# Feed-forwards of a decoder trunk: seven rounds for eight, the order of the block products, and where the second matrix's weights are loaded

## The chip, the core and the metric

One NeuronCore of a Trainium2 chip runs the whole kernel in one launch. The time is the device time of one execution in microseconds (us), and smaller is better. The engines are named as in the profile: PE multiplies matrices, PEld loads its weights, DVE, ACT and POOL work on vectors, SP issues most of the transfers.

## The reference, cut to what matters

The program is one step of a two-layer decoder trunk for 512 prompt tokens and 32 sample tokens. Each layer holds two feed-forwards around a mixer, so there are four in all; the mixers, the shared keys and values and the conditioning are not touched by the change.

```python
def swiglu(u, w_up, w_down):
    a, b = jnp.split(u @ w_up, 2, axis=-1)
    return (jax.nn.silu(a) * b) @ w_down
...
u = modulate(h, P['g_norm'][layer, 0], mod[:, 0, 0], mod[:, 0, 1])
h = h + 0.5 * mod[:, 0, 2][:, None, :] * swiglu(u, P['w_ffn_up'][layer, 0], P['w_ffn_down'][layer, 0])
```

The model width is 1024, the width between the two matrices is 2816, that is 22 columns of 128; all data are float32.

## The kernel before, in words

**Layout.** Activations lie transposed, features on the partitions, in eight blocks of 128 features by 544 tokens. The tokens are taken in two halves of 272. Every operand of a matmul is split into a high part (an ACT cast) and a low part (a DVE subtraction), and each product is three matmuls: high by high, high by low, low by high. The helpers `halves` (line 157 and 158) and `acc3` (lines 176 to 178) do this, so nearly all of these instructions carry those lines; the tiles tell them apart: `p` is a bank of a block product, `pd` a bank of the second matrix, `pa` and `pb` banks of the plain way.

**One feed-forward.** `ffn_seven` is called four times ("00", "02", "10", "12" in time order). A "pair" q is the 128 columns of a and the 128 columns of b that belong together. The first three pairs (0 to 2) are computed plainly. From pair 3 on, `seven` computes a 2 by 2 block product (feature half by token half) with seven products of 12 matmuls each instead of eight, from sums of weights (S1 to S4) and sums of activations (T1 to T4). The sums of activations are made by DVE and ACT while PE works on the plain pairs (`inputs`, `last_input`); T2 and T4 are the tiles `th`, `tl`, and T3 is written over a quarter of `uh`, `ul`.

**Weights of the first matrix.** `load(q)` issues two transfers of 512 KB into the four `raw` buffers (`rua`, `rub`). `stage(q, 0..4)` turns them into operands: step 0 is two POOL operations (lines 639 and 640), step 1 splits A11 and A12 and lets POOL make two more sums, steps 2 to 4 split the summed blocks. Split operands lie in six `hi` and six `lo` buffers. During pair q the steps of pair q + 1 are emitted, between the products of pair q, and `load(q + 2)` behind step 3.

**The second matrix.** The finished pairs (`gh`, `gl`, five or six buffers, parameter `slots`; "00" and "02" have five) are collected in rounds. While a round's pairs are computed, the 16 blocks (8 feature blocks by 2 token halves) of the round before it are emitted between the products by `between`, spread over n products, n at most 7 times (slots - 3). A block of a round of three pairs is 9 matmuls, of a round of two 6. `residual` then adds the bank onto `h` (DVE, line 398; for the second token half also lines 401 and 403 on DVE and POOL). `down_weights(r, m2)` loads and splits the weights of two feature blocks of round r (`rd`, `hd`, `ld`); `blocks` calls it one group ahead. `low` makes the low part of a finished pair on POOL, in the last round on DVE (line 677).

**The end.** The last round's 16 blocks run alone, all of the first token half, then all of the second. Behind each half come the squares for the norm (ACT line 351, sums on POOL line 355), `stats` (PE line 364), a reciprocal root on DVE, `spread` (PE line 342, `rb`), and `make_u`, the input of the next stage. In "00" and "02" a piece of conditioning work (`held`) is emitted ahead of `stats`. The last feed-forward ends in `store` instead.

**Order.** The source gives an order and so a priority; a planner puts the instructions of each engine into their final order by its own costs and gives out the buffers, so that a line moved in the source moves in a queue only as far as the planner follows. Each engine then runs its queue strictly in order.

Of the kernel before, what the change touches and what calls it, by code (L numbers as in the profile page):

```python
# [27 lines left out]
NQ = FF // P  # L28
# [58 lines left out]
def cols(t, nk, w):  # L87
    return t[:, 0:nk * w].rearrange("p (k c) -> p k c", k=nk)
# [11 lines left out]
def trunk_kernel(ctx: ExitStack, tc: tile.TileContext, a, out, dbg=None, stop=None):  # L100
# [9 lines left out]
    def mm_bank(name):  # L110
        return pp.tile([P, 512], F32, tag="mm", name=name, bufs=5)
# [8 lines left out]
    def raw_tile(name, dt=F32):  # L120
        return wp.tile([P, 1040], dt, tag="raw", name=name, bufs=4)

    def hi_tile(name, dt=F32R):
        return wp.tile([P, 1040], dt, tag="hi", name=name, bufs=6)

    def lo_tile(name, dt=F32R):
        return wp.tile([P, 1040], dt, tag="lo", name=name, bufs=6)
# [28 lines left out]
    def halves(hi, lo, src):  # L156
        S.copy(hi, src)  # L157
        V.tensor_tensor(out=lo, in0=src, in1=hi.bitcast(F32), op=ALU.subtract)  # L158
# [14 lines left out]
    def acc3(ps, steps, first=True, last=True):  # L173
        n = len(steps)
        for i, (wh, wl, xh, xl) in enumerate(steps):
            PE.matmul(ps, lhsT=wh, rhs=xh, start=first and i == 0, stop=False)  # L176
            PE.matmul(ps, lhsT=wh, rhs=xl, start=False, stop=False)  # L177
            PE.matmul(ps, lhsT=wl, rhs=xh, start=False, stop=last and i == n - 1)  # L178
# [136 lines left out]
    for t in range(5):  # L315
        n = P if t < 4 else NS
# [196 lines left out]
    def ffn_seven(name, l, s, gate, after_half, steps=(), final=False, first=None, held=(), slots=6, late=False):  # L513
# [8 lines left out]
            for _ in range(max(total * ticks[0] // n_ticks, min(total, ticks[0], 4)) - (total - len(steps))):  # L522
                steps.pop(0)()
        rounds, q0 = [], 0
        for n in (3, 3, 3, 3, 3, 3, 2, 2):
            rounds.append(list(range(q0, q0 + n)))
            q0 += n
        assert q0 == NQ
        H2 = NB // 2
        with tc.tile_pool(name="ffn" + name, bufs=1) as fp:  # L530
# [52 lines left out]
            def operand(i, kh=0, half=0):  # L583
                if i in th:
                    return th[i], tl[i]
                return quarter(uh, kh, half), quarter(ul, kh, half)
            B11, B21, B22 = operand(0, 0, 0), operand(0, 1, 0), operand(0, 1, 1)
            T1, T2, T3, T4 = operand(1), operand(2), operand(0, 0, 1), operand(4)
# [30 lines left out]
            def load(q):  # L619
                if q < NQ:  # L620
                    raws[q] = [raw_tile(f"ru{x}{name}_{q}") for x in "ab"]
                    for raw, c0 in zip(raws[q], (q * P, FF + q * P)):
                        SP.dma_start(out=cols(raw, NB, P), in_=wu[:, c0:c0 + P].rearrange("(k p) c -> p k c", p=P))

            def stage(q, step):
                if q >= NQ:
                    return
                ra, rb_ = raws[q]
                a11, a12, a21, a22 = ra[:, 0:W4], ra[:, W4:2 * W4], rb_[:, 0:W4], rb_[:, W4:2 * W4]
                o = ops.setdefault(q, {})  # L630

                def pair():
                    return hi_tile(f"hu{name}_{q}_{step}"), lo_tile(f"lu{name}_{q}_{step}")

                def view(t, i):
                    return tuple(x[:, i * W4:(i + 1) * W4].rearrange("p (k c) -> p k c", k=H2) for x in t)
                if step == 0:
                    o["s3"] = tmp.tile([P, 512], F32, tag="w2", name=f"s3{name}_{q}", bufs=1)
                    G.tensor_tensor(out=o["s3"][:], in0=a11, in1=a21, op=ALU.subtract)  # L639
                    G.tensor_tensor(out=a21, in0=a21, in1=a22, op=ALU.add)  # L640
                elif step == 1:
                    t = pair()
                    halves(t[0][:, 0:2 * W4], t[1][:, 0:2 * W4], ra[:, 0:2 * W4])
                    o["A11"], o["A12"] = view(t, 0), view(t, 1)
                    G.tensor_tensor(out=a11, in0=a21, in1=a11, op=ALU.subtract)  # L645
                    G.tensor_tensor(out=a12, in0=a12, in1=a11, op=ALU.subtract)
                elif step == 2:
                    t = pair()
                    halves(t[0][:, W4:2 * W4], t[1][:, W4:2 * W4], o["s3"][:])
                    halves(t[0][:, 0:W4], t[1][:, 0:W4], a11)  # L650
                    o["S2"], o["S3"] = view(t, 0), view(t, 1)
                elif step == 3:
                    t = pair()
                    halves(t[0][:, 0:2 * W4], t[1][:, 0:2 * W4], rb_[:, 0:2 * W4])
                    o["S1"], o["A22"] = view(t, 0), view(t, 1)
                else:
                    t = pair()
                    halves(t[0][:, 0:W4], t[1][:, 0:W4], a12)
                    o["S4"] = view(t, 0)

            def product(q, n, w, x):
                ps = mm_bank(f"p{n}{name}_{q}")
                acc3(ps[:, 0:HA], [(w[0][:, k], w[1][:, k], x[0][:, k], x[1][:, k]) for k in range(H2)])
                return ps[:, 0:HA]

            def part(q, what):
                return tmp.tile([P, HA], F32, tag={"u": "nv", "c": "sq", "a": "acc"}[what[0]], name=f"{what}{name}_{q}", bufs=2 if what[0] == "a" else 3)

            def plus_ps(q, what, ps, x):
                d = part(q, what)  # L670
                V.tensor_tensor(out=d[:], in0=ps, in1=x[:], op=ALU.add)
                return d
# [6 lines left out]
            def seven(q, between):  # L679
                o = ops[q]  # L680
                g_tiles(q)
                stage(q + 1, 0)
                s1 = part(q, "u1")
                S.copy(s1[:], product(q, 1, o["A11"], B11))
                between()
                u2 = plus_ps(q, "u2", product(q, 6, o["S2"], T2), s1)
                between()
                a0 = plus_ps(q, "a0", product(q, 2, o["A12"], B21), s1)
                S.activation(a0[:], a0[:], AF.Silu)
                stage(q + 1, 1)  # L690
                between()
                u3 = plus_ps(q, "u3", product(q, 7, o["S3"], T3), u2)
                stage(q + 1, 2)
                between()
                p5 = product(q, 5, o["S1"], T1)
                c22 = plus_ps(q, "c22", p5, u3)
                u4 = plus_ps(q, "a4", p5, u2)
                between()
                c21 = plus_ps(q, "c21", product(q, 4, o["A22"], T4), u3)
                V.tensor_tensor(out=c21[:], in0=c21[:], in1=a0[:], op=ALU.mult)  # L700
                (t0, t1), (t2, t3_) = HALF
                low(q, t0, t1, c21)
                stage(q + 1, 3)
                load(q + 2)
                between()
                c12 = plus_ps(q, "c12", product(q, 3, o["S4"], B22), u4)
                S.activation(c12[:], c12[:], AF.Silu)
                V.tensor_tensor(out=c12[:], in0=c12[:], in1=c22[:], op=ALU.mult)
                low(q, t2, t3_, c12)
                stage(q + 1, 4)  # L710
                between()


            def down_weights(r, m2):
                if r >= len(rounds) or (r, m2) in down_w:
                    return
                qs = rounds[r]
                n = len(qs)
                src = wd[qs[0] * P:(qs[-1] + 1) * P, 2 * m2 * P:2 * (m2 + 1) * P].rearrange("(q p) c -> p q c", p=P)
                raw = raw_tile(f"rd{name}_{r}_{m2}")  # L720
                SP.dma_start(out=cols(raw, n, 2 * P), in_=src)
                hi, lo = hi_tile(f"hd{name}_{r}_{m2}"), lo_tile(f"ld{name}_{r}_{m2}")
                halves(hi[:, 0:2 * n * P], lo[:, 0:2 * n * P], raw[:, 0:2 * n * P])
                down_w[r, m2] = (cols(hi, n, 2 * P), cols(lo, n, 2 * P))
# [61 lines left out]
            last_input()  # L786
            stage(plain, 3)
            stage(plain, 4)
            load(plain + 1)
            down_weights(0, 0)  # L790
            for r in range(1, len(rounds)):
                todo = blocks(r - 1)
                n, done, gone = min(7 * len(rounds[r]), 7 * (slots - 3)), [0], [0]

                def between():
                    done[0] += 1
                    while gone[0] < min(2 * NB * done[0] // n, 2 * NB):
                        next(todo)
                        gone[0] += 1
                    tick()  # L800
                for q in rounds[r]:
                    seven(q, between)
                for _ in todo:
                    pass
            r = len(rounds) - 1
# [771 lines left out]
    if stop == "kv":  # L1577
        return

    ffn_seven("10", 1, 0, mod(1, 0, 2), after("11", mod(1, 1, 0), mod(1, 1, 1)))  # L1580
    dump("h3", h[:])

# [314 lines left out]
```

## Time and profile before

| what | value |
|---|---|
| median of 3 runs | 2404.79 us (2399.41 to 2405.72) |
| the profiled execution | 2402.91 us, its span 2401.1 us |
| mean granted TensorE clock | 0.980 of full speed |
| PE busy | 2298.5 us, 96% of the span |
| PEld busy | 2141.6 us, 89% |
| DVE busy | 1828.6 us, 76% |
| ACT busy, POOL busy | 982.0 us and 923.0 us |

The span runs from the first to the last instruction; what lies around it is 1.8 us. The times of the rows below are microseconds from the start of the span.

A row of busy time by stretch holds the stretch, its length, then busy us (and instructions) of PE, PEld, DVE, ACT and POOL, the granted clock as a share of full speed, the DMA share and GB/s. The four insides summed there are 100 to 448, 795 to 1152, 1352 to 1672 and 2060 to 2378 us. A timeline row holds start, us, engine, line, operation, output and inputs, shape, count, and in brackets the idle time before it with what ended it.

### The profile page before, as it was taken

To read this page: it belongs to the slowest core of one execution; us is meant where nothing else is said; L and a number is where in the kernel's file an instruction comes from. 1 tells how busy PE (TensorE), PEld (TensorE's weight loads), DVE (VectorE), ACT (ScalarE), POOL (GpSimd) and SP (SyncE) were. 2 spreads that over 40 slices of the span, in tenths; PEclk is the share of its full clock that TensorE was granted. 3 is DMA by queue.
4 is the path that set the end of the run, shared out by engine and by line. 5 is a ranking of instruction groups with operands and counts; after the bars stand their busy time and mean duration, and the time that the engine had idled before them with its cause. 6 is when DMAs were issued, how large, how long until landed. Compare 5 with 4: busy or idle time off the path is not lost. (4 is left out here: it accounts for less than half of the span.)

```text
span 2401.1 us, 49301 instructions
## 1 busy us (share of the span) xinstructions
PE 2298.5 (96%) x19292; PEld 2141.6 (89%) x19292; DVE 1828.6 (76%) x3881; ACT 982.0 (41%) x1831; POOL 923.0 (38%) x960
## 2 busy tenths in 40 slices
PE   7999999998999999999989999999999799999999
PEld 6899999987979999999769999999796479999999
DVE  6887777749556987777795988888757667888887
ACT  3343333444533443333524444434436544444432
POOL 0355544207102365444241355543324212455452
PEclk8999999999999999999999999999899899999999
DMA  8535555322172445555467233332146751233322
GB/s 306 172 124 193 192 187 178 114 69 62 54 219 64 141 129 181 187 174 174 144 203 246 81 104 94 99 94 88 47 111 185 157 164 52 78 104 89 102 84 78
DMA packets 356894, 319.45 MB, mean 133 GB/s; under 512 B 25247, under 2 KB 317949, under 8 KB 356614
## 3 DMA queue, kind: packets, MB, share of 16 engines
q1 hardware_dynamic: 341734, 300.24, 40.0%
q0 software_dynamic: 14928, 16.06, 3.0%
q8 instruction: 152, 2.49, 0.4%
q14 instruction: 80, 0.66, 0.1%
HBM read 298.17 MB, written 18.38 MB: 132 GB/s over the span
## 5 line engine op out<-in xcount | busy, mean ns | idle before, releaser
L178 PE MATMUL pd<-gh,ld 128*128 128x272 f32 x1408 | 408.6, 290 | 3.3 <-DVE ld L158 3.3
L176 PE MATMUL pd<-gh,hd 128*128 128x272 f32 x1408 | 409.2, 291 | 2.5 <-ACT hd L157 2.5
L177 PE MATMUL pd<-gl,hd 128*128 128x272 f32 x1408 | 409.3, 291 | 2.2 <-POOL gl L677 2.2
L176 PE MATMUL p<-uh,hu 128*128 128x272 f32 x1216 | 351.8, 289 | 0.0
L177 PE MATMUL p<-ul,hu 128*128 128x272 f32 x1216 | 350.9, 289 | 0.0
L178 PE MATMUL p<-uh,lu 128*128 128x272 f32 x1216 | 350.8, 288 | 0.0
L158 DVE TENSOR_TENSOR lu<-rua,hu 128x512 fp32r<-128x512 f32 (+1 forms) x228 | 272.2, 1194 | 45.9 <-ACT hu L157 37.7
L157 ACT CAST hu<-rua 128x512 fp32r<-128x512 f32 (+1 forms) x228 | 174.0, 763 | 290.4 <-PE p L177 131.8
L398 DVE SCALAR_TENSOR_TENSOR h<-pd,mods,h 128x240 f32<-128x240 f32 (+1 forms) x512 | 240.5, 476 | 49.7 <-PE pd L178 48.9
L178 PEld LDWEIGHTS pd<-gh,ld 128*128 128x128 f32 x1408 | 268.3, 191 | 3.9 <-DVE ld L158 3.9
L176 PEld LDWEIGHTS pd<-gh,hd 128*128 128x128 f32 x1408 | 268.4, 191 | 3.5 <-ACT hd L157 2.7
L177 PEld LDWEIGHTS pd<-gl,hd 128*128 128x128 f32 x1408 | 268.5, 191 | 3.0 <-POOL gl L677 3.0
L176 PE MATMUL p<-th,hu 128*128 128x272 f32 x912 | 264.5, 290 | 1.8 <-ACT th L157 1.8
L178 PE MATMUL p<-th,lu 128*128 128x272 f32 x912 | 264.2, 290 | 0.0
L177 PE MATMUL p<-tl,hu 128*128 128x272 f32 x912 | 264.0, 290 | 0.2 <-DVE tl L158 0.2
L403 POOL TENSOR_TENSOR h<-h,gs 128x32 f32<-128x32 f32 x256 | 127.9, 499 | 333.9 <-DVE gs L401 333.6
L176 PEld LDWEIGHTS p<-uh,hu 128*128 128x128 f32 x1216 | 229.3, 189 | 6.2 <-issue 2.1
L177 PEld LDWEIGHTS p<-ul,hu 128*128 128x128 f32 x1216 | 229.4, 189 | 0.0
L178 PEld LDWEIGHTS p<-uh,lu 128*128 128x128 f32 x1216 | 228.9, 188 | 0.0
L639 POOL TENSOR_TENSOR s<-rua,rub 128x512 f32<-128x512 f32 x76 | 115.1, 1514 | 244.6 <-DMA rub<-in_w_ffn_up_dram 131.3
L645 POOL TENSOR_TENSOR rua<-rub,rua 128x512 f32<-128x512 f32 x76 | 101.2, 1332 | 225.0 <-DVE lu L158 130.2
L176 PEld LDWEIGHTS p<-th,hu 128*128 128x128 f32 x912 | 172.4, 189 | 6.1 <-ACT th L157 2.0
(543 smaller groups left out, 6007.4 us busy)
## 6 DMA issues: line engine op xcount, KB each, us to landing
adaw<-in_w_ada_dram SPq DMA_DIRECT2D x128, 512.0 KB, 4.5
rua<-in_w_ffn_up_dram SPq DMA_DIRECT2D x88, 512.0 KB, 3.9
rub<-in_w_ffn_up_dram SPq DMA_DIRECT2D x88, 512.0 KB, 3.8
rd<-in_w_ffn_down_dram SPq DMA_DIRECT2D x96, 384.0 KB, 3.3
adah<-in_w_ada_dram SPq DMA_DIRECT2D x16, 512.0 KB, 6.3
adaw<-in_w_ada_kv_dram SPq DMA_DIRECT2D x16, 512.0 KB, 8.2
rd<-in_w_ffn_down_dram SPq DMA_DIRECT2D x32, 256.0 KB, 2.7
kp<-in_cache_k_dram SPq DMA_DIRECT2D x16, 512.0 KB, 11.9
```

What stands on the lines that cost most here:

```text
L157: S.copy(hi, src)
L158: V.tensor_tensor(out=lo, in0=src, in1=hi.bitcast(F32), op=ALU.subtract)
L176: PE.matmul(ps, lhsT=wh, rhs=xh, start=first and i == 0, stop=False)
L177: PE.matmul(ps, lhsT=wh, rhs=xl, start=False, stop=False)
L178: PE.matmul(ps, lhsT=wl, rhs=xh, start=False, stop=last and i == n - 1)
L398: V.scalar_tensor_tensor(out=h[:, m, t0:p1], in0=ps[:, 0:n], scalar=mods[:, gate + m, 0:1], in1=h[:, m, t0:p1], op0=ALU.mult, op1=ALU.add)
L403: G.tensor_tensor(out=h[:, m, TP:T], in0=h[:, m, TP:T], in1=st[:], op=ALU.add)
L639: G.tensor_tensor(out=o["s3"][:], in0=a11, in1=a21, op=ALU.subtract)
L645: G.tensor_tensor(out=a11, in0=a21, in1=a11, op=ALU.subtract)
```

## The change

The rounds are cut differently: six of three pairs and one of four, instead of six of three and two of two. In `seven` the product of A12 comes second, ahead of the one of S2 and T2, and stage step 1 of the next pair moves with it. The first weights of the second matrix for round 0 are asked for ahead of `load(plain + 1)` and not behind it. For the last round, `down_weights` is called for its first group ahead of the last pair and for its second group within it.

```diff
-        for n in (3, 3, 3, 3, 3, 3, 2, 2):
+        for n in (3, 3, 3, 3, 3, 3, 4):
...
                 S.copy(s1[:], product(q, 1, o["A11"], B11))
                 between()
-                u2 = plus_ps(q, "u2", product(q, 6, o["S2"], T2), s1)
-                between()
                 a0 = plus_ps(q, "a0", product(q, 2, o["A12"], B21), s1)
                 S.activation(a0[:], a0[:], AF.Silu)
                 stage(q + 1, 1)
                 between()
+                u2 = plus_ps(q, "u2", product(q, 6, o["S2"], T2), s1)
+                between()
                 u3 = plus_ps(q, "u3", product(q, 7, o["S3"], T3), u2)
                 stage(q + 1, 2)
+                if q == NQ - 1:
+                    down_weights(len(rounds) - 1, 1)
                 between()
...
             stage(plain, 4)
+            down_weights(0, 0)
             load(plain + 1)
-            down_weights(0, 0)
...
                 for q in rounds[r]:
+                    if q == NQ - 1:
+                        down_weights(r, 0)
                     seven(q, between)
```

## Rows read from the trace of the kernel before

**Rows 1.** The page's engines: busy us, share of the span, instructions.
```profile
PE 2298.5 (96%) x19292; PEld 2141.6 (89%) x19292; DVE 1828.6 (76%) x3881; ACT 982.0 (41%) x1831; POOL 923.0 (38%) x960
```

**Rows 2.** Busy time by engine: third feed-forward inside, and sum over all four insides.
```profile
1352.00:1672.00 320.00, 318.90 (x2534) 318.47 (x2534) 270.66 (x464) 130.74 (x219) 154.39 (x159) 1.00 0.32 96
...
sum 1343.00, PE 1338.52 PEld 1308.19 DVE 1087.53 ACT 528.51 POOL 641.60; mean PE 334.63 PEld 327.05 DVE 271.88 ACT 132.13 POOL 160.40
```

**Rows 3.** Timeline of PE, first feed-forward, pair 3: start, us, idle before.
```profile
87.14 0.39 PE L176 MATMUL pd<-gh,hd 128*128 128x272 f32 x1 [2.45 <-ACT hd L157]
...
90.43 0.60 PE L178 MATMUL pd<-gh,ld 128*128 128x272 f32 x1 [2.78 <-DVE ld L158]
...
98.85 0.29 PE L176 MATMUL p<-uh,hu 128*128 128x272 f32 x1
```

**Rows 4.** Timeline of SP's issues, first feed-forward.
```profile
72.85 0.39 SPq L623 DMA_DIRECT2D rua<-in_w_ffn_up_dram  x1
73.33 1.77 SPq L623 DMA_DIRECT2D rub<-in_w_ffn_up_dram  x1
81.52 3.00 SPq L721 DMA_DIRECT2D rd<-in_w_ffn_down_dram  x2
```

**Rows 5.** Busy time, as in rows 2, around that wait.
```profile
84.50:88.50 4.00, 0.70 (x4) 0.30 (x2) 3.97 (x6) 1.15 (x2) 2.39 (x2) 1.00 0.73 215
88.50:95.30 6.80, 4.87 (x21) 4.87 (x22) 5.03 (x12) 2.27 (x5) 0.00 (x0) 0.50 0.37 111
```

**Rows 6.** Timeline of DVE, first feed-forward, pair 3.
```profile
83.99 0.43 DVE L546 TENSOR_TENSOR x<-uh,ul 128x272 f32<-128x272 f32 x1
84.45 1.39 DVE L539 TENSOR_TENSOR x<-x,x 128x272 f32<-128x272 f32 x1
...
92.56 0.43 DVE L158 TENSOR_TENSOR ul<-x,uh 128x272 fp32r<-128x272 f32 x1
```

**Rows 7.** Timeline of POOL, first feed-forward, stage 0 of pair 4.
```profile
81.95 3.60 POOL L639 TENSOR_TENSOR s<-rua,rub 128x512 f32<-128x512 f32 x1 [5.82 <-DMA rub<-in_w_ffn_up_dram]
```

**Rows 8.** Timeline of PE, last feed-forward, pair 3.
```profile
2057.79 0.47 PE L176 MATMUL p<-th,hu 128*128 128x272 f32 x1 [1.80 <-ACT th L157]
...
2063.88 0.29 PE L176 MATMUL p<-uh,hu 128*128 128x272 f32 x1
```

**Rows 9.** Busy time, as in rows 2, around that wait.
```profile
2058.00:2061.40 3.40, 3.20 (x14) 2.95 (x14) 3.37 (x8) 1.89 (x4) 0.00 (x0) 0.50 0.81 251
```

**Rows 10.** Timeline of DVE, last feed-forward: the last piece of T3.
```profile
2059.02 1.28 DVE L539 TENSOR_TENSOR ul<-t,uh 128x1088 fp32r<-128x1088 f32 x1
```

**Rows 11.** Waits of PE, third feed-forward, 1340 to 1702: us, times, longest.
```profile
PE st L364 <- POOL sq L355: 3.5, 2, 1.9
PE rb L342 <- DVE diag L341: 1.9, 1, 1.9
PE pd L177 <- POOL gl L677: 0.6, 1, 0.6
PE pd L178 <- DVE ld L158: 0.5, 1, 0.5
```

**Rows 12.** Busy time, as in rows 2, at the third feed-forward's end.
```profile
1682.50:1689.30 6.80, 6.80 (x34) 6.80 (x33) 2.38 (x13) 3.10 (x6) 1.53 (x4) 0.50 0.00 0
1696.20:1706.30 10.10, 9.67 (x32) 8.41 (x33) 7.84 (x27) 5.50 (x11) 1.91 (x4) 0.50 0.10 10
```

**Rows 13.** Busy time, as in rows 2, at the first feed-forward's end.
```profile
453.70:457.10 3.40, 3.40 (x17) 3.40 (x16) 2.17 (x14) 1.70 (x3) 0.50 (x2) 0.50 0.98 362
```

**Rows 14.** Busy time, as in rows 2, second feed-forward, a pair without blocks.
```profile
894.00:905.00 11.00, 11.00 (x90) 11.00 (x89) 8.37 (x15) 4.07 (x8) 8.41 (x8) 1.00 0.64 232
```

**Rows 15.** Timeline of DVE, third feed-forward, last pair: c21 and its low part.
```profile
1668.99 0.44 DVE L671 TENSOR_TENSOR c<-p,u 128x272 f32<-128x272 f32 x1 [1.01 <-PE p L178]
...
1671.09 0.44 DVE L677 TENSOR_TENSOR gl<-c,gh 128x272 fp32r<-128x272 f32 x1
```

**Rows 16.** Groups of DVE, third feed-forward, 1350 to 1680: busy, mean ns.
```profile
L398 DVE SCALAR_TENSOR_TENSOR h<-pd,mods,h 128x272 f32<-128x272 f32 x64 | 31.0, 492 | 1.5 <-PE pd L178 1.3
```

## The prediction, made before the changed kernel ran

> **What bounds the kernel now.** I read the page's engine table first: PE is busy 96% of the span, DVE 76% [rows 1]. That share is an average, so the next view is busy time by stretch. Inside the four feed-forwards, 1343 us together, PE is busy 1338.5 us, and the clock stands at its upper level of 2.4 GHz [rows 2]: 4.5 us are to be had there. Such a stretch also gives the price of a matmul: 320 us for 2534 of them, 0.126 us each. So a product of 12 is 1.5 us, a block of 9 is 1.1 us, and the change can only earn what PE loses at the edges of the feed-forwards. There I read the waits of PE and the timeline, with the granted clock beside them.
>
> At the first feed-forward's start PE stands 2.45 us for the high part of the second matrix's first weights and 2.78 us for the low part [rows 3]; behind that the clock is at 1.2 GHz for 6.8 us [rows 5]. The cause is in SP's queue: the two loads of pair 4 go at 72.85 and 73.33, the second matrix's first load at 81.52 [rows 4]. At the last feed-forward's start PE stands 1.80 us in the middle of a product with T2 [rows 8], and the clock falls for 3.4 us [rows 9]. At the third one's end the waits sum to 5.4 us (statistics twice, the spread matrix once) [rows 11], with 6.8 and 10.1 us at 1.2 GHz [rows 12].
>
> **What does not change.** A block holds 3 matmuls for each pair of its round, so 16 blocks over 22 pairs stay 1056 matmuls a feed-forward, and the products stay too. Seven rounds for eight take away 16 evacuations a feed-forward, 64 in all; at 0.49 us [rows 16] that is 31 us of DVE, besides the small ones for the samples on DVE and POOL. I cost this at nothing: inside a feed-forward PE's matmuls cover DVE's work already [rows 2], and a shorter queue behind a cover gives no time; where DVE sets the pace, at the starts, no evacuation is saved. Bytes are the same, in 28 transfers of the second matrix for 32.
>
> **Step 1 of the next pair, one product earlier.** It issues a cast, a subtraction and two POOL sums. Its buffers come free when products 1 and 2 are done, which is now also a product earlier. The evacuation of product 6 stands behind its subtraction on DVE; only the next sum needs that, 1.5 us later, and five banks cover it. Nothing gained, nothing lost: if that cover fails it is at most the 0.44 us of one evacuation [rows 15] for a pair, and 19 pairs in four feed-forwards would show it as 33 us, which the third pairs of the second feed-forward, full at 11.00 of 11.00 us without any block [rows 14], speak against.
>
> **Start of the first feed-forward.** The wait begins at 84.7 (87.14 less 2.45) and product 7 starts at 98.85 [rows 3]. Between lie three blocks and two products, 51 matmuls, 6.4 us; so 7.7 us are lost. Asked for ahead of pair 4's loads, the weights take the buffer that went to pair 4's first half at 72.85, nine microseconds sooner, and both splits can be done when product 1 ends. What is late next is DVE: it is busy 3.97 of 4.00 us there [rows 5], and T3, which product 7 needs, is ready at 93.0 [rows 6]. Four evacuations (two products, two blocks) that were behind it now come ahead, 4 x 0.44 = 1.8 us, so 94.8; the last quarter of T3 is used 9 matmuls (1.1 us) into the product, so product 7 may start at 93.7, a gain of 5.1. Bounds: 0 if the planner leaves DVE's order as it is, 7.7 if T3 comes first. I take 4.5. Behind the moved load on SP is pair 4's second half; it gets its buffer at 81.5 and not at 73.3, and POOL's step 0 for pair 4 moves from 81.95 [rows 7] to about 90 (the 8.6 us from issue to 81.95 kept). Pair 4's products start near 100, so that is covered.
>
> **Start of the last feed-forward.** The wait begins at 2056.0, product 7 starts at 2063.88 [rows 8]; 33 matmuls lie between, 4.2 us, so 3.7 us are lost. The product of A12 uses plain activations and now fills 1.5 us, and a block 1.1 us more, before T2 is touched, so both the wait and the dip should go. Next late is T3, ready at 2060.3 [rows 10], or 2062.1 behind four evacuations: a gain of 3.6 or 1.8. I take 2.5, bounds 0 and 3.7. The third feed-forward loses 0.5 us to the low part of the first weights [rows 11]; that goes.
>
> **Ends.** The last round's blocks grow from 6 matmuls to 12, a token half from 6 to 12.1 us. At the third one's end, POOL's sums of squares and DVE's root chain for the first half, which PE overtook, then lie under matmuls: the spread's 1.9 us goes, and the two waits for squares fall from 3.5 us to about 1.1 us each (an estimate: the last evacuation, 0.49, and a square of like length), 1.3 us. The dips, 16.9 us, cost half, 8.4 us; at the first feed-forward's end the dip behind the statistics is 3.4 us [rows 13], and two such would cost 3.4, 5.0 less. Upper bound 8.2, lower 0; I take 4.5, as no held work stands here ahead of the statistics. The ends of the first and the second have held work and one short dip: 1 together (0 to 3.4). The last has no statistics: 0.
>
> **Round boundaries.** The wait of 0.6 us for POOL's low part [rows 11] (two of these, in the third and the last) is where a round's first block comes behind one product, because a round of two spreads the blocks over 14 products. Over 21 it comes later: 1, bounds 0 and 1.2. On the other side, no blocks of an older round are left behind the last pair. From its sum c21 to its low part takes 2.5 us [rows 15]; product 3 and the first three pairs' matmuls of the first block cover 2.6. A wider split in that queue may uncover 0.7, the width doubling from one of 512 columns, in each of four: I charge 1 (0 to 2.8).
>
> **Sum.** 4.5 + 2.5 + 0.5 + 4.5 + 1 + 1 - 1 = 13.0 us. The profiled execution took 2402.9 us, so **2389.9, say 2390 us**. It stands 1.9 us under the median of the runs, 2404.8. All lower bounds together give 2406, all upper ones 2378. Own range 2383 to 2397. A measurement of this kernel tells 0.3%, 7.2 us, from no change.
>
> **Rivals.**
> *Given back at the same edges (0.24).* The planner leaves SP's or DVE's order, or DVE, full at the starts [rows 5, 9], makes PE wait for T3 instead, with a dip again; at the third end the dips stay. Left are the spread's 1.9, 0.5, 1 and 1 at the first start, less 1: 3.4 us, **2399**. For it speaks DVE's full row; against it, that T3's end, as reckoned above, still leaves a gain at both starts.
> *All of it comes (0.08).* Both starts without a wait and the shorter dips: 7.7 + 3.7 + 0.5 + 8.2 + 1 + 1.2 = 22 us, **2381**.
> *Slower (0.08): POOL in DVE's way at the starts.* Beside POOL's step 0 a DVE sum takes 1.39 us where its neighbour takes 0.43 [rows 6, 7]. Pair 4's second half now lands later, so step 0 falls into the stretch in which PE waits for T2 and T3. If its 3.6 us all reach PE, with a dip of 3.4 us at half speed, that is 5.3 at each of four starts, 21 us, less 5 from the ends: **2419**. It decides if T2 is still unfinished when that half lands. Against it: in the first feed-forward step 0 already sits in that stretch and would leave it. The Trainium skill (SBUF — State Buffer, section Who interferes with whom) says that a DVE instruction with two SBUF inputs and a GpSimd instruction that reads SBUF share a port that one holds whole while the other is blocked; the 1.39 us agree, and by that rule this rival is what a later step 0 does.
>
> **Chances and range.** Forecast 0.60, rivals as given: faster 0.60 + 0.08 = 0.68, same 0.24, slower 0.08. The range runs from 2379, near the sum of the upper bounds, to 2403, past the first rival; the slower one is left out.
>
> **What would show it.** Right: SP issues `rd` ahead of pair 4's second load; no wait for `hd`, `ld` or `th` in the four starts, and product 7 of pair 3 near 94 and near 2061.5 (less what was gained before); at the third end no wait at `rb` and fewer than 10 us at 1.2 GHz; insides as full as now. Wrong: PE waiting for `uh`, `ul` at product 7; a new wait at the first block of the last round; POOL's line 639 beside slow DVE sums at a start; dips of the old length.

## The result and the profile after

The changed kernel takes 2379.45 us (median of 4 runs, 2373.35 to 2383.6) beside 2404.31 us (4 runs, 2399.41 to 2405.72) of the kernel before on the same chip: ratio 0.9898, 95% interval 0.9879 to 0.9917. It is faster by 24.9 us where 13 was forecast; it stands at the lower edge of the range (2379 to 2403) and below the forecast's own 2383 to 2397. The profiled execution took 2383.6 us, the slowest of the four, and its span of 2381.8 is 19.3 us shorter than the span before; the places below are reckoned on these two spans, by the start of the same matmul in each, and the other 5.6 us are in no row.

| stretch of the span | forecast | measured |
|---|---|---|
| start of the first feed-forward | 4.5 | 3.7 |
| start of the third | 0.5 | -0.4 |
| start of the last | 2.5 | 3.2 |
| end of the first and of the second | 1 together | -1.8 and +0.9 |
| end of the third, to the first matmul of `fq` (of `hTq`) | 4.5 | 10.4 (13.4) |
| end of the last | 0 | 0.1 |
| inside the four | 1 - 1 | 1.1, 2.0, 0.1, 1.0 |

A start runs from pair 3's first matmul to that of product 7, an inside from there to the last pair's last matmul. An end runs from that one to the first of `gv` (first), `pa` (second) or `hTq` (third), which are banks of the mixer or of the next plain pairs, and to the last one of `pd` (last); the matmuls of the second matrix that lie in it are taken off at 0.126 us each: 192 after, 108 before, the 96 of the last round and 12 of the round ahead of it. What is left to 19.3 is -4.1 us in the mixers and the plain pairs: 1.0 in the first mixer, 1.5 each in the plain pairs of the second and of the last feed-forward, where stretches at 1.2 GHz (3.4 us at 756.9 and at 1999.3) stand that the kernel before does not have there. The second end's row is the least sure. It is 165 to 174 us long, with most of a mixer in it: at the first matmul of `pus`, a bank of that mixer 60 to 65 us behind the last pair, the change is 5.4 us ahead, and the mixer behind that gives 4.5 back, amid falls of the clock that stand elsewhere in each run.

The page's engines after, the answer to [rows 1]: PE's work is the same, DVE has 96 instructions less.

```profile
PE 2289.9 (96%) x19292; PEld 2136.8 (90%) x19292; DVE 1741.8 (73%) x3785; ACT 976.4 (41%) x1815; POOL 908.4 (38%) x912
```

**The first start.** The timeline of PE in pair 3 of the first feed-forward, then SP's issues ahead of it (columns as in [rows 3, 4]).

```profile
86.37 0.39 PE L178 MATMUL pd<-gh,ld 128*128 128x272 f32 x1 [1.33 <-DVE ld L158]
...
91.11 0.39 PE L176 MATMUL pd<-gh,hd 128*128 128x272 f32 x1 [1.35 <-ACT gh L157]
92.23 0.39 PE L177 MATMUL pd<-gl,hd 128*128 128x272 f32 x1 [0.73 <-DVE gl L158]
...
95.21 0.29 PE L176 MATMUL p<-uh,hu 128*128 128x272 f32 x1
```

```profile
72.95 0.38 SPq L723 DMA_DIRECT2D rd<-in_w_ffn_down_dram  x1
73.43 0.61 SPq L623 DMA_DIRECT2D rua<-in_w_ffn_up_dram  x1
81.58 0.37 SPq L623 DMA_DIRECT2D rub<-in_w_ffn_up_dram  x1
```

The second matrix's load has taken the place of pair 4's first half, as reckoned, and the second half goes 8 us later. The wait for `hd` is gone, that for `ld` is 1.33 us and no longer 2.78 [rows 3]; two new ones stand behind it, for a finished plain pair. Product 7 starts at 95.21 where 98.85 stood. The prediction had POOL's step 0 near 90, with the 8.6 us from issue kept; it starts 3.9 us behind the issue of the second half, at 85.46. Why the pair is late is read on three engines, here ACT, DVE and POOL in their timelines.

```profile
90.63 0.42 ACT L157 CAST gh<-g 128x272 fp32r<-128x272 f32 x1 [2.32 <-DVE g L612]
```

```profile
86.23 2.97 DVE L158 TENSOR_TENSOR ul<-x,uh 128x272 fp32r<-128x272 f32 x2
...
90.18 0.42 DVE L612 TENSOR_TENSOR g<-g,pb 128x272 f32<-128x272 f32 x1
```

```profile
85.46 1.99 POOL L639 TENSOR_TENSOR s<-rua,rub 128x512 f32<-128x512 f32 x1 [9.26 <-DVE x L546]
87.53 1.37 POOL L640 TENSOR_TENSOR rub<-rub 128x512 f32<-128x512 f32 x1
```

POOL's step 0 for pair 4 now falls on the splits of T3: two of them take 2.97 us where one took 0.43 [rows 6]. The finished pair's product (line 612) stands behind them on DVE, ACT's cast behind that, and PE behind the cast. The Trainium skill (SBUF — State Buffer, section Who interferes with whom) says that DVE with two SBUF inputs and a GpSimd that reads SBUF share a port that one of them holds alone; the 2.97 us agree with it. So the slower rival's mechanism was there, at a price of some 2 us (1.35 + 0.73). It is not new, though. In the kernel before, the same step 0 stretches two DVE sums a little earlier (the first is in [rows 6]), and the pair's product is no sooner:

```profile
85.88 1.39 DVE L546 TENSOR_TENSOR x<-uh,ul 128x272 f32<-128x272 f32 x1
...
90.29 0.43 DVE L612 TENSOR_TENSOR g<-g,pb 128x272 f32<-128x272 f32 x1
```

There it was hidden behind the wait for `ld`; with the weights early it is what PE waits for. That PE would wait 2 us less without POOL beside DVE is argued from these rows; no run takes POOL away.

**The third end.** Waits of PE from 1640 to 1730, the answer to [rows 11], and busy time by stretch, the answer to [rows 12].

```profile
PE st L364 <- POOL sq L355: 1.5, 1, 1.5
PE rb L342 <- DVE diag L341: 0.5, 1, 0.5
PE fq L979 <- DVE lfq L158: 0.3, 1, 0.3
```

```profile
1657.20:1687.00 29.80, 27.82 (x222) 27.25 (x220) 20.54 (x55) 12.93 (x27) 11.63 (x17) 1.00 0.06 18
1687.00:1714.00 27.00, 27.00 (x184) 22.07 (x185) 22.87 (x86) 15.04 (x28) 6.59 (x12) 1.00 0.32 99
```

The same stretch of the kernel before, from the last matmul of the last pair to the first of `fq`:

```profile
1670.90:1700.50 29.60, 24.27 (x153) 23.54 (x152) 20.15 (x59) 16.36 (x32) 15.26 (x25) 0.81 0.15 39
```

The stretches are equally long, but the new one holds 192 matmuls of the second matrix and not 108, which is 10.6 us more work. The granted clock was 0.81 there and is 1.00. Both falls to 1.2 GHz, 16.9 us together, are gone, though a wait of 1.50 us is left.

Why PE no longer overtakes the statistics is read on POOL, which sums the squares of the first half's blocks (line 355); before, then after:

```profile
1676.35 5.01 POOL L355 TENSOR_TENSOR sq<-sq,sq 128x272 f32<-128x272 f32 x5 [1.31 <-ACT sq L351]
```

```profile
1663.39 0.78 POOL L355 TENSOR_TENSOR sq<-sq,sq 128x272 f32<-128x272 f32 x1 [0.72 <-ACT sq L351]
1664.96 0.77 POOL L355 TENSOR_TENSOR sq<-sq,sq 128x272 f32<-128x272 f32 x1 [0.79 <-ACT sq L351]
```

Before, five sums stand back to back, 1.0 us each, where a block of 6 matmuls takes PE 0.76 us. After, a block takes 1.5 us and POOL waits 0.7 to 0.8 us for each next square. The last rounds also differ in who makes a pair's low part (DVE in the last round, POOL in the others), but no low part stands in POOL's queue here in either kernel.

**The ends of the first two.** A wait for `adat` that the kernel before does not have at this place stands there now, with the clock behind it. Timeline of PE, then busy time by stretch, first feed-forward's end:

```profile
456.79 0.29 PE L176 MATMUL gq<-uh,hgq 128*128 128x272 f32 x1
460.21 0.69 PE L243 MATMUL adat<-cst,adar 128*128 128x128 f32 x2 [3.13 <-ACT adar L240]
```

```profile
459.90:470.10 10.20, 9.89 (x45) 9.90 (x46) 6.42 (x25) 1.17 (x3) 0.00 (x0) 0.50 0.15 37
```

The kernel before waits as long at this end, for other tiles (440 to 494):

```profile
PE st L364 <- POOL sq L355: 1.7, 2, 0.9
PE gq L176 <- ACT uh L157: 1.5, 1, 1.5
```

So what the first end loses is not the wait itself, 3.13 us for 3.2, but the fall of 10.2 us behind it where 3.4 us stood [rows 13]. At the second's end the wait for `adat` is 2.33 us, with 6.8 us at 1.2 GHz. `adat` is the transposing of the second held piece of conditioning work, `adar` the copy that ACT makes for it. ACT's timeline shows where that copy stands:

```profile
457.67 0.43 ACT L351 ACTIVATE sq<-h 128x272 f32<-128x272 f32 x1 [1.38 <-POOL h L403]
458.01 0.73 ACT L157 CAST hgv<-rgv 128x672 fp32r<-128x672 f32 x1
458.65 0.52 ACT L391 ACTIVATE uh<-nv,mods 128x272 fp32r<-128x272 f32 x1
459.07 0.41 ACT L351 ACTIVATE sq<-h 128x272 f32<-128x272 f32 x1
459.39 0.51 ACT L391 ACTIVATE uh<-nv,mods 128x272 fp32r<-128x272 f32 x1
459.81 0.35 ACT L240 COPY adar<-ada 128x256 f32<-128x256 f32 x1
```

The copy stands behind the squares of the second half's blocks, and each square waits for POOL's sum of its block's samples (line 403); the mixer's matmuls wait behind the transposes on PE.

**The last start.** Timeline of PE; the wait for `th` of [rows 8] is gone, and product 7 starts 7.5 us behind the end of the plain pairs (2038.19), where it was 10.7 (2053.18 to 2063.88).

```profile
2045.33 0.40 PE L177 MATMUL pd<-gl,hd 128*128 128x272 f32 x1 [0.46 <-DVE gl L158]
...
2045.69 0.29 PE L176 MATMUL p<-uh,hu 128*128 128x272 f32 x1
```

### The profile page after: what moved, and what is told of

It reads as the page before. It is cut to its first block, busy times and chain, and to the rows that moved or that the text cites. A ratio compares the mean times of both kernels' runs of the same rounds, so it can differ in the third digit from the quotient of the medians.

```text
span 2381.8 us, 48923 instructions
## 1 busy us (share of the span) xinstructions
PE 2289.9 (96%) x19292; PEld 2136.8 (90%) x19292; DVE 1741.8 (73%) x3785; ACT 976.4 (41%) x1815; POOL 908.4 (38%) x912
## 5 line engine op out<-in xcount | busy, mean ns | idle before, releaser
L398 DVE SCALAR_TENSOR_TENSOR h<-pd,mods,h 128x272 f32<-128x272 f32 (+1 forms) x448 | 211.7, 476 | 69.9 <-PE pd L178 68.4
L158 DVE TENSOR_TENSOR lu<-rua,hu 128x512 fp32r<-128x512 f32 (+1 forms) x228 | 232.2, 1019 | 35.9 <-ACT hu L157 32.6
L639 POOL TENSOR_TENSOR s<-rua,rub 128x512 f32<-128x512 f32 x76 | 122.9, 1617 | 288.8 <-DMA rub<-in_w_ffn_up_dram 112.7
L403 POOL TENSOR_TENSOR h<-h,gs 128x32 f32<-128x32 f32 x224 | 115.0, 513 | 244.9 <-DVE gs L401 239.5
L645 POOL TENSOR_TENSOR rua<-rub,rua 128x512 f32<-128x512 f32 x76 | 107.5, 1415 | 185.4 <-DVE lu L158 104.9
```

The source lines that it names most:

```text
L398: V.scalar_tensor_tensor(out=h[:, m, t0:p1], in0=ps[:, 0:n], scalar=mods[:, gate + m, 0:1], in1=h[:, m, t0:p1], op0=ALU.mult, op1=ALU.add)
L403: G.tensor_tensor(out=h[:, m, TP:T], in0=h[:, m, TP:T], in1=st[:], op=ALU.add)
```

## The experiments

The theory was that each part pays at its own edge, and that the rounds pay because longer last blocks cover the statistics. Its rivals were that the parts only pay together, that the 64 saved evacuations count after all, or that the early loads of the last round do. The last runs ask what the new waits at the first two ends cost, and whether that can be had back.

**Parts alone.** *The rounds alone (e1):*

```diff
-        for n in (3, 3, 3, 3, 3, 3, 2, 2):
+        for n in (3, 3, 3, 3, 3, 3, 4):
...
+                if q == NQ - 1:
+                    down_weights(len(rounds) - 1, 1)
...
+                    if q == NQ - 1:
+                        down_weights(r, 0)
```

> The kernel before with the rounds alone: seven of them, with the two early calls for the last round's weights, and neither the order of the products nor the first weights moved. Theory (each edit earns at its own edge, and the parts add): the whole gain at the third feed-forward's end, some 13 us from the last product to the mixer's first matmul with no stretch at 1.2 GHz there, and nothing at the starts, where the waits for hd and ld (5.2 us, first feed-forward) and for th (2.0 us, last one) are still there; 2404 - 15 = 2389 us, between 2384 and 2394. Rival (the ends gain only together with DVE being ahead from the starts): within 5 us of before.

Measured 2388.67, ratio 0.9944 (0.9927 to 0.996), 13.6 us under the kernel before of its chip (2402.32). Its third end gains 10.4 us to `fq`, as the whole change's does, and PE's waits there are the same to the tenth; the waits at both starts stay.

```profile
PE st L364 <- POOL sq L355: 1.5, 1, 1.5
PE rb L342 <- DVE diag L341: 0.5, 1, 0.5
```

*The order alone (e2):*

```diff
-                u2 = plus_ps(q, "u2", product(q, 6, o["S2"], T2), s1)
-                between()
                 a0 = plus_ps(q, "a0", product(q, 2, o["A12"], B21), s1)
                 S.activation(a0[:], a0[:], AF.Silu)
                 stage(q + 1, 1)
                 between()
+                u2 = plus_ps(q, "u2", product(q, 6, o["S2"], T2), s1)
+                between()
```

> The kernel before with the product of A12 put second, and nothing else. Theory: the wait for th at the last feed-forward's start (2.0 us and 3.4 us at 1.2 GHz) goes, 3 us, and the waits for hd and ld in the first one stay; 2401 us. Rival (DVE is the bound there, the wait moves to hd, ld or T3): 2404 us, with a wait of 1 to 2 us for another tile at the same place.

Measured 2395.09, ratio 0.9971 (0.9957 to 0.9984): 7.2 us, more than twice the forecast. The last start gains 2.1 us: the wait for `th` is gone, and the first block waits 1.2 us for its weights' low part instead. The insides of the four gain 1.8, 2.0, 0.9 and 0.7, together 5.4: PE waits there for nothing any more. In the kernel before these are the waits (first, then second feed-forward, 111 to 440 and 821 to 1149; the third and the last have only POOL's low part, 0.6 and 0.7):

```profile
PE adat L243 <- ACT adar L240: 1.0, 1, 1.0
PE pd L177 <- POOL gl L677: 0.5, 1, 0.5
```

```profile
PE adat L243 <- ACT adar L240: 0.8, 1, 0.8
PE pd L177 <- POOL gl L677: 0.4, 1, 0.4
```

They sum to 4.0 us of the 5.4. At the third end all stays, waits and clock, here from its last blocks on:

```profile
1679.00:1706.00 27.00, 22.91 (x100) 19.90 (x100) 18.71 (x72) 11.51 (x23) 10.75 (x19) 0.74 0.12 26
```

*The first weights alone (e3):*

```diff
+            down_weights(0, 0)
             load(plain + 1)
-            down_weights(0, 0)
```

> The kernel before with the second matrix's first weights asked for ahead of pair 4, and nothing else. Theory: the waits for hd and ld at the first feed-forward's start fall from 5.2 us to under 2, 4 us in all, and the wait for th at the last one's start stays; 2400 us. Rival (POOL's step 0 then falls among DVE's sums): slower than before by 3 us or more, with DVE sums of over 1 us beside line 639 at the starts.

Measured 2400.78, ratio 0.9989 (0.9974 to 1.0004): 1.5 us, too little to tell from nothing. The first start gains 2.3 us in its rows. The waits are those of the whole change to the hundredth (1.33, 1.35, 0.73), but the clock falls behind them, which it does not in the whole change:

```profile
91.50:94.90 3.40, 3.30 (x14) 3.31 (x15) 2.42 (x8) 0.71 (x2) 0.25 (x1) 0.51 0.60 174
```

The expectation had the wait for `th` at the last start staying. It goes here too, with the products in their old order: `hd` is split early, ACT casts the last piece of T2 1.8 us behind pair 3's first matmul and not 4.1, and product 7 starts 7.5 us behind that matmul (2051.86), as in the whole change, which is 3.2 us sooner than before:

```profile
2059.36 0.29 PE L176 MATMUL p<-uh,hu 128*128 128x272 f32 x1
```

The insides of e3 are 1.5 us longer than before, so that little of this is left in its time.

*The whole change without the two early calls for the last round (e4):*

```diff
-                if q == NQ - 1:
-                    down_weights(len(rounds) - 1, 1)
...
-                    if q == NQ - 1:
-                        down_weights(r, 0)
```

> The changed kernel without the two early calls for the last round's first and second weights. Theory (the planner asks for them when buffers are free, and the calls in the source move little): as the changed kernel within 3 us, 2377 to 2383. Rival (without them the last round's first block comes before its weights): a wait of 3 to 5 us for hd or ld at the first block of the last round in each feed-forward, with stretches at 1.2 GHz, 12 to 20 us over the changed kernel.

Measured 2377.8, ratio 0.9897 (0.9878 to 0.9917), the whole change's own. The calls are worth nothing that can be told from noise. The three parts sum to 13.6 + 7.2 + 1.5 = 22.3 us, the whole change gives 24.9, and the intervals overlap, so the times add. The places do not: at the last start the order alone gains 2.1 and the first weights alone 3.2, and both together gain 3.2.

**Why the rounds pay.** Three other cuts of the 22 pairs, each put into the whole change. *Eight rounds, the last of four (e5):* as many evacuations as before, last blocks as in the change.

```diff
-        for n in (3, 3, 3, 3, 3, 3, 4):
+        for n in (3, 2, 2, 3, 3, 3, 2, 4):
```

> The changed kernel with eight rounds again, of 3, 2, 2, 3, 3, 3, 2 and 4 pairs: the evacuations of the kernel before, the last round of the changed one. Theory (the length of the last round's blocks lets POOL's sums of squares and DVE's root chain keep up, and that is what the third feed-forward's end gains): as the changed kernel, 2379 us within 4, no stretch at 1.2 GHz at the third end. Rival (the 16 evacuations less per feed-forward are what pays): 2379 + 14 = 2393 us.

Measured 2393.84, ratio 0.9956 (0.994 to 0.9972): the rival's number, but not by the rival's cause. The third end is close to the change's, with the same two waits, though with a fall of 3.4 us where the theory had none. The loss is at the rounds of two in the third and in the last feed-forward: beside the change, their insides lose 3.2 and 5.2 us and their starts 1.9 and 2.6. Waits of PE, 1340 to 1720:

```profile
PE pd L177 <- POOL gl L677: 2.9, 2, 2.8
PE st L364 <- POOL sq L355: 1.5, 1, 1.5
PE pd L176 <- ACT hd L157: 0.9, 1, 0.9
PE rb L342 <- DVE diag L341: 0.5, 1, 0.5
```

PE waits 2.76 us for POOL's low part of the pair just finished, the wait that the kernel before has at 0.6 us [rows 11]. So this cut does not tell the evacuations from such waits; the next two do.

*Seven rounds, the four early (e6)* and *six rounds, the last four of four (e8);* in both n counts the buffers that the round before leaves:

```diff
-        for n in (3, 3, 3, 3, 3, 3, 4):
+        for n in (3, 4, 3, 3, 3, 3, 3):      # e8: (3, 3, 4, 4, 4, 4)
...
-                n, done, gone = min(7 * len(rounds[r]), 7 * (slots - 3)), [0], [0]
+                n, done, gone = min(7 * len(rounds[r]), 7 * (slots - max(3, len(rounds[r - 1])))), [0], [0]
```

> The changed kernel with seven rounds of 3, 4, 3, 3, 3, 3 and 3 pairs: the evacuations of the changed kernel, a last round of three. (The number of products that a round's blocks are spread over counts the round before, so that buffers come free in time.) Theory of the block length: a block of 9 matmuls takes 1.1 us, between the 0.75 of before and the 1.5 of the changed kernel, and POOL takes some 0.8 to 1.0 us for a square, so a part of the wait and of the slow stretch comes back: 3 to 8 us over the changed kernel, 2382 to 2387. Rival (fewer evacuations): 2379 us within 3.

> The changed kernel with six rounds, of 3, 3, 4, 4, 4 and 4 pairs: 16 evacuations less again in each feed-forward, the same last round. (The blocks of a round of four are spread over fewer products, so that buffers come free in time: 14 products with six buffers, 7 with five.) Theory (evacuations lie under PE's matmuls and are worth nothing): 2379 us within 4. Rival (fewer evacuations pay, or DVE's relief): 5 us or more under the changed kernel.

Measured: e6 2390.76, ratio 0.9943 (0.9923 to 0.9962); e8 2379.59, ratio 0.9897 (0.9871 to 0.9922). Six rounds have 16 evacuations a feed-forward less than the change and take its time, within some 6 us. Its first two feed-forwards have new waits (their insides are 4.6 us behind the change's), so the third and the last show it best: there the insides are within 0.7 us of the change's, with 16 evacuations less in each. So no sign is left that evacuations count. With a last round of three, 11 us of the change's gain are missing (0.9943 for 0.9898), though the count of rounds is the same. That is 4 us more than the theory's interval allows, and only a part of it is the last round's: by the rows 6.0 us are lost at the third end and 6.1 inside the four, where the new cut brings waits for POOL's low part of up to 1.2 us in the first two, 0.8 in the third and 0.7 in the last. The waits at the third end are these:

```profile
PE fq L978 <- ACT uh L391: 2.2, 2, 1.3
PE fq_s L966 <- POOL us L383: 1.9, 1, 1.9
PE st L364 <- ACT sq L351: 0.4, 1, 0.4
PE rb L342 <- DVE diag L341: 0.4, 1, 0.4
PE st L364 <- POOL sq L355: 0.2, 1, 0.2
```

The cuts side by side at that end. The stretch runs from the start of the last pair's last matmul to the first of `hTq`; the third column takes off the second matrix's matmuls in it, at 0.126 us each, and the others hold PE's waits and the granted clock in the stretch:

```
                matmuls    stretch, us   less these, us  waits, us   clock
before, e2        108      59.5, 59.5    45.9, 45.9      6.8, 7.0    0.86
e3                108      57.4          43.8            6.3         0.88
e6                153      57.7          38.5            5.1         0.97
e5                192      58.3          34.1            2.0         0.97
e1, e8, after     192      56.7 to 56.8  32.5 to 32.6    2.0         1.00
```

What the end costs beyond these matmuls falls with the length of the last round, 5 to 7 us from 108 to 153 and 4 to 6 more to 192, and not with the count of rounds: e1, e6 and the change have seven, e5 eight, e8 six. The waits and the clock account for it: with them taken off too, the time at 1.2 GHz (17 us before, 14 in e3, 3.4 in e6 and e5) at half, every row comes to between 30.4 and 31.7 us. A last round of three has most of the clock back but not the waits, most of which lie behind the statistics there; one of four has both back. The same cut differs by up to 2 us (e3 beside the kernel before: its first fall of the clock is 3.4 and not 6.8 us long).

**The wait at the first two ends.** *The whole change with the second held piece issued after the fifth block of the second half (e7),* and with it *after the third (e10);* the same edit *in the kernel before (e9).*

```diff
                     if half and m >= 2 and us_:
                         us_.pop(0)()
-                if held:
+                    if half and m == NB - 4 and held:      # e10: NB - 6
+                        held.pop(0)()
+                if held and not half:
                     held.pop(0)()
```

> The changed kernel with the second held piece of conditioning work issued after the fifth block of the last round's second half, in the first and second feed-forward, instead of behind the last block. Theory (in the changed kernel its transposes stand in PE's queue ahead of the mixer's matmuls and wait 3.1 and 2.3 us for a copy that lies behind the squares and the next input on ACT, and the clock falls after that for 10.2 and 6.8 us): these waits go; a wait of 1 to 1.5 us for the last squares, which the piece covered, comes instead; 6 us under the changed kernel, 2370 to 2376. Rival (the wait for the squares and the clock's fall come in any case): 2379 us within 3.

> The changed kernel with the second held piece after the third block of the second half (two blocks, 24 matmuls of 0.126 us, 3 us ahead of the place in e7). Theory (the transposes wait for the ACT copies behind the squares and the input of the mixer, some 2.1 us late in e7): with 3 us more of blocks behind the place PE no longer waits for adat, the clock falls less, and the time is 2 to 5 us under e7's distance to the changed kernel, ratio to the kernel before 0.985 to 0.987. Rival (the planner or ACT's queue moves the copies with the piece, so that the wait only moves): the same as e7, ratio 0.987 to 0.988, with a wait of about 2.1 us for adat still there.

> The kernel before with one edit alone: in the last round of a feed-forward the second held piece of conditioning work is issued after the fifth block of the second token half. Theory (what the early piece gives back is a wait that the new rounds made, since their last blocks end closer to the piece): the kernel before has no such wait at the first end, so nothing comes of it, within 0.15% of the kernel before, about 2400 to 2406. Rival (the place of the piece is worth the same whatever the rounds are): 6 us less than the kernel before, about 2398, with the stretches at 1.2 GHz behind the first and second ends shorter.

Measured: e7 2373.3, ratio 0.9868 (0.9841 to 0.9895); e10 2367.76, ratio 0.9852 (0.9831 to 0.9873), the fastest of all, 36 us under the kernel before of its chip (2403.5). In e7 the wait for `adat` does not go, as its theory had it; it is 2.1 us at both ends, amid the blocks. The second end gains 6.1 us over the change (the 6.8 us at 1.2 GHz right behind it are gone), the first 0.8. In e10 the waits are 0.7 and 0.6, and the first end gains 4.3 us, the second 5.2. Of the second end's gains 3.1 (e7) and 3.7 us (e10) are there at the first `pus`; the rest is in the mixer behind, where e4 too, with the change's own place of the piece, is 3.6 us ahead of the change. The rows of e10, ACT first and then PE:

```profile
448.43 0.35 ACT L240 COPY adar<-ada 128x256 f32<-128x256 f32 x1
```

```profile
448.83 0.44 PE L243 MATMUL adat<-cst,adar 128*128 128x128 f32 x2 [0.65 <-ACT adar L240]
```

```profile
447.90:484.00 36.10, 35.04 (x275) 34.15 (x274) 23.58 (x65) 15.62 (x36) 7.78 (x16) 1.00 0.05 12
```

Reckoned from the start of the last pair's last matmul, the copy starts 27.0 us later (448.43 - 421.44) and not 34.9 (459.81 - 424.92), and the clock stays at 1.00 behind the transposes; one fall of 3.4 us is left amid the blocks, at 438.7. e9 took 2398.26 beside 2403.5, ratio 0.9979 (0.9966 to 0.9992), which is near the rival's number. Its rows don't show that gain: its span is 2401.1 us like that of the kernel before, nothing is gained at the first end, and 0.6 us at the second. But the profiled execution, 2402.83 us, is the slowest of its twelve, and what made the others shorter stays open. So, by the ratios, the early piece is worth some 7 (e7) to 11 us (e10) behind the longer rounds, where e7's interval still overlaps with the change's and e10's does not. That it is worth nothing behind the shorter rounds is not shown.

## Why the prediction was right in its direction and short in its size

*What bounds.* PE at the edges of the feed-forwards: right. The insides after are as full as before (1307.2 of 1309 us busy, against [rows 2]), and the 64 saved evacuations were costed at nothing; e8 shows no sign of another price.

*The step that was mis-sized* is the third end's term: "The dips, 16.9 us, cost half, 8.4 us; at the first feed-forward's end the dip behind the statistics is 3.4 us [rows 13], and two such would cost 3.4", and its "Upper bound 8.2". It measured 10.4 us to `fq` and 13.4 to `hTq`. The falls did not shrink to the length of another end's: they went altogether, 8.4 us in place of 5.0. The waits for `rb` and the squares went from 5.4 to 2.0 us, 3.4 where the term had 3.2. That is 11.8 of the 13.4. Another 1.4 are waits of the kernel before behind the first `fq` (0.5 for `us`, 0.5 for `uh`, 0.4 for `ul`), which the change does not have and the term did not count. And of the sum, 8.2, only some half was taken, as no held work stands there; the run shows no such loss. A length borrowed from another end was used as a floor, and it was none.

*The first start* (4.5, measured 3.7) was near in price and right in what it removes. What is late next was DVE, as said, but not at T3: a finished plain pair behind T3's splits, which POOL stretched: step 0 came upon them at 85.46, and not near 90. *The last start* (2.5, measured 3.2) was near in price but only in part right in cause: it was put down to the order of the products, and e3 has all of it with the old order, from the first weights' place, to which the prediction gave nothing there. The order alone gave 7.2 us, where its term has 2.5 in this start: it also takes away the short waits inside the four feed-forwards, of which the text priced two, as a gain of the rounds, and those for `adat` not at all.

*The ends of the first two* (1 together, measured -1.8 and +0.9): the text said only that they have held work and one short dip. It did not ask when that work's own copy on ACT becomes ready once the blocks take longer; by e10 the copy's place costs 8 to 9.5 us in the two ends, as the second is read at `pus` or at `pa`.

*The third start* (0.5, measured -0.4): the short wait for the low part of the first weights is still there. *Round boundaries and the last pair* (1 and -1; the insides measured 4.2): the last pair uncovered nothing, and of POOL's low part a wait of 0.7 us is left in the third, at another round.

*The sum* came nearer than its terms. The third end gave 8.9 us more than its term and the insides 4.2 more; the ends of the first two, the third start and the mixers and plain pairs, for which there was no term, took 6.9 back (1.9, 0.9 and 4.1).

*Rivals.* "Given back at the same edges" failed at the third end, where the clock did not fall again. "All of it comes" has the time, 2381, but not the way: at the first start half of the 7.7 came, the first end lost, and the third gave more than its bound. The slower rival's mechanism was there and cost some 2 us at one start and not 5.3 at four: no fall of the clock came with it, and at the other three starts PE waits 0, 0.5 (`ld`) and 0.5 us (`gl`).

## What to carry to other kernels

Where blocks of the second matrix end a stage ahead of a reduction with its chain across other engines, give the last round more columns: the same matmuls then cover the chain, and in this kernel the length of the last round set the price of that end, not the count of rounds. A short round elsewhere can cost as much (e5). Read a part that is tried alone at every edge and not only at its own: the first weights' place paid at a start where the order of the products was to pay. When work is moved behind such an edge, follow what stands in the queue ahead of the next stage too, and ask for each piece on which engine its last input is made and behind what. A fall of the clock is to be priced both as staying and as going altogether, not by the length that it has at another place.

## What was not expected of the hardware

The same three waits of PE (1.33, 1.35 and 0.73 us within 7 us) were followed by 3.4 us at 1.2 GHz in e3 and by none in the changed kernel, and a single wait of 1.50 us at the third end by none, where 3.13 us at the first end was followed by 10.2 us. So these runs do not let the clock's answer be read from the length of a wait alone. And two POOL operations of 3.4 us stretched two DVE splits from 0.43 us each to 2.97 together, some 2.1 us, and the delay stood in the way of PE by way of two other engines.
